# Hybrid encoder block on one core: the conv branch's layer norm in channels-by-tokens layout, attention scores over the allowed keys only

## The chip, the cores and the metric

The kernel runs on 1 core of one Trainium2 chip. TensorE (PE) multiplies matrices: it holds one operand as weights (the loads are the rows of PEld) and streams the other through, with results in PSUM, eight banks of 128 partitions by 512 fp32 numbers. VectorE (DVE), ScalarE (ACT) and GpSimd (POOL) work on tiles of up to 128 partitions in SBUF or PSUM. SyncE (SP) and ACT issue the DMAs, the copies between device memory and SBUF. Each engine works through its own instruction list in order and waits on semaphores of the others. The metric is the device time of one execution, in microseconds (us); lower is better.

## The reference

One layer of an encoder, for 1 sequence of 1024 tokens with 1024 features, in float32:

```python
h = rms_norm(x, norm1_g)
z = h @ w_in                                  # 2560 columns: a, gate, q, k, v, 512 each
# conv branch (512 channels)
u = a * sigmoid(gate)
y = depthwise_conv(u, dw_kernel) + dw_bias    # 31 taps over the tokens, centred
xc = y - mean(y, channels)
y = xc * rsqrt(mean(xc * xc, channels) + 1e-6) * ln_g + ln_b
conv_out = silu(y)
# attention branch: 8 heads of 64, tokens on a grid of 16 rows x 64 columns
q, k = rms_norm per head
# each query attends to a window of 8 rows x 16 columns, clamped inside the grid
s = q . k / 8 + rpb[row offset, column offset]
attn_out = softmax(s) @ v
x = x + concat(conv_out, attn_out) @ w_out
h = rms_norm(x, norm2_g)
x = x + (silu(h @ w_gate) * (h @ w_up)) @ w_down      # 2816 hidden features
```

A key column can be used by a query only if it lies in the query's 16 columns, and likewise for rows; all other keys of a tile get a table entry of -1e30 in place of the bias and so a weight of 0.

## The kernel before

The order of every engine's instructions is the order in which the program is written (the scheduler is set to manual). PE work is interleaved by hand: `proj` and the input projections emit their matmuls, and after each three of them (a `mac`: an fp32 product as three products of split halves, hi·hi, hi·lo, lo·hi, L115 to L117) call `weave()`, which pops one closure from the list `woven` and emits it there. `split` (L107 on ACT, L111 on DVE or POOL) makes the hi and lo halves that `mac` takes: ACT rounds to hi, the other engine subtracts.

SBUF buffers come from pools by size: `G` 21 of 128x1024, `H` 7 of 128x4096, `R` 4 of 128x1024, `ST` 5 of 128x512, `SM` 12 small ones. PSUM has `mm` (4 banks), `tp` (2 banks) and `cv` (one tile of 2 banks). A tile that takes a buffer waits until the readers of the tile before it in that buffer are done. A DMA also waits until the DMA issued eight before it on its completion semaphore has landed.

The stages, in us of the profiled execution: first norm, k projection and the GLU (0 to 95); q projection, the bias tables and most of the conv taps (95 to 200); the value projection with the first scores (200 to 235.3); the attention loop (235.3 to 294.8); the rest of attention, the conv layer norm and the first part of the output projection (294.8 to 337.4); the second part (337.4 to 420); the FFN's up half (420 to 730) and down half (730 to 1029).

*Conv branch.* `u[c]` (c = 0 to 3) is a tile of 128 channels by 1024 tokens. DVE does most of the taps (L363, one instruction of 128x1009 or more for each tap and channel block), ACT and POOL the others (L385 to L389), and DVE adds both sums into `u[c]` (L368). In the layer norm, `conv_T(t)` (L824) turns 128 tokens with 4 transposes of `u` on PE into one tile `y` of tokens by 512 channels; DVE takes its mean and variance (L831, L832), ACT the root (L833), DVE the reciprocal (L843); ACT (L852) or DVE (L848) writes the normalised rows `xh`. `conv_silu(h, c)` (L857) turns 4 blocks of `xh` back with 4 transposes into `z`, 128 channels by 512 tokens; ACT applies gain, bias and Silu (L858), and `split` makes `cm[h]`, the left operand of the output projection `pj`. There are 8 `conv_T` and 8 `conv_silu`, each a closure in `woven`, popped between the matmuls of the output projection whose left operand is the attention output `at`.

*Attention.* A step `s_` is 128 queries (8 grid rows of 16 columns), `order` lists the 8 steps by half of the rows `rh` and column block `cb`. `WIN` gives the key columns of each block: 24, 32, 32, 24. `AR` = 12 is the number of key rows. An index `i` is a step and a pair of heads, 32 in all. `score_mm(i)` (L680) makes 2 products of 128 queries by 12·24 = 288 or 12·32 = 384 keys; `score_max` (L693) adds the table `tab` and takes the row maximum; `score_exp` (L698) is ACT's exponential with its sum; `score_norm` (L707 on DVE, L709 on POOL) scales; `flip(i)` (L720) makes 3 transposes for each head (keys onto partitions, 4 grid rows of keys, 96 or 128, at a time); `flip_out` copies them to SBUF (L727 on DVE, L729 on ACT); `weigh(i)` (L739) multiplies with the value rows `vw`. Each weighing product and each score product shows as two matmul records.

*Value rows.* The value projection writes `vd` in device memory (8 tiles of 128 tokens, by ACT's queue, L447); `load_vw` (L660) reads windows of it back through SP's queue, one DMA for each grid row in a group of 4, of 24 or 32 tokens, for one or two groups at a time.

Of the kernel before, what the change touches and what calls it, by code (L numbers as in the profile page):

```python
# [25 lines left out]
AR = 12  # L26
SIDE = (16, 17, 18, 19, 20, 21, 22)
WIN = ((0, 24, 8), (8, 32, 0), (24, 32, 0), (40, 24, 0))
# [42 lines left out]
def build(ctx, tc, a):  # L71
# [206 lines left out]
    t1 = [dr.tile([NH, 16, 15, ncol], F32, name=f"t1{ty}") for ty, ncol in enumerate((24, 32, 24))]  # L278
    tf = {(rh, ty): dr.tile([16, 8, NH, AR * t1[ty].shape[-1]], F32, name=f"tf{rh}{ty}")
# [71 lines left out]

    def conv_taps():
        for c in range(4):
# [14 lines left out]
            dve.tensor_tensor(uc, acc, aside[c][0], OP.add)  # L368
            yield True
# [132 lines left out]
    aside_dma = []  # L502

    def bias_tables():
        neg = G("neg")
        pool.memset(neg, NEG)

        def fill1(ty):
            n = 15 * t1[ty].shape[-1]
            nc.sync.dma_start(t1[ty].rearrange("h j u b -> (h j) (u b)"), neg[:, :n])  # L510

        def fill2(rh, ty):
            n = 3 * AR * t1[ty].shape[-1] if ty != 1 else 2 * AR * 32
            for o in range(0, NH * AR * t1[ty].shape[-1], n):
                w = min(n, NH * AR * t1[ty].shape[-1] - o)
                nc.sync.dma_start(tf[rh, ty].rearrange("j i h c -> (j i) (h c)")[:, o:o + w], neg[:, :w])
# [6 lines left out]
        def rows_of(rh, ty, i):  # L523
            ncol = t1[ty].shape[-1]
# [113 lines left out]
    def table(rh, ty):  # L638
        n = AR * t1[ty].shape[-1]
        src = tf[rh, ty].rearrange("j i h c -> (j i) (h c)")  # L640
        if rh == 0 and ty == 0:
            parts = [(G(f"tab{k}")[:, :n * min(3, NH - 3 * k)], 3 * k) for k in range(3)]
# [10 lines left out]

    def load_vw(cb, *gs):
        c0, ncol, _ = WIN[cb]
        if gs[0] % 2 == 0:
            vwt[cb, gs[0] // 2] = G(f"vw{cb}{gs[0]}").rearrange("p (g d) -> p g d", d=512)
        w = vwt[cb, gs[0] // 2]
        for r in range(4):
            nc.sync.dma_start(w[r * ncol:(r + 1) * ncol, gs[0] % 2:gs[-1] % 2 + 1, :],  # L660
                              vd.rearrange("(g r c) d -> r c g d", r=4, c=GW)[r, c0:c0 + ncol, gs[0]:gs[-1] + 1, :])
        for g in gs:
            vw[cb, g] = w[:4 * ncol, g % 2, :]


# [4 lines left out]

    def score_mm(i):
# [3 lines left out]
        c0, ncol, _ = WIN[cb]  # L675
        s2 = cv(f"s{i}") if i > 0 and i % 2 == 0 else None
        out = []
        for hh in range(2):
            s = (mm(f"s{i}{hh}") if s2 is None else lr(s2)[hh])[:, :AR * ncol]
            pe.matmul(s, qT[hh * HD:(hh + 1) * HD, hp, t * P:(t + 1) * P],  # L680
                      k4[hh * HD:(hh + 1) * HD, hp, rh * 4:rh * 4 + AR, c0:c0 + ncol], start=True, stop=True)
# [3 lines left out]
    def score_max(i, hh, s):  # L685
        s_, hp = divmod(i, 4)
        rh, cb = order[s_]
        if i not in es:
            et[i] = G(f"e{i}").rearrange("p (h n) -> p h n", h=2)
            es[i] = et[i][:, :, :AR * WIN[cb][1]]  # L690
# [21 lines left out]
    def flip(i):  # L712
        s_, hp = divmod(i, 4)
        m = 4 * WIN[order[s_][1]][1]
# [3 lines left out]
        for hh, pt in enumerate(pp[i]):  # L718
            for g in range(3):
                pe.transpose(pt[:m, g * P:(g + 1) * P], es[i][:, hh, g * m:(g + 1) * m], ident)  # L720

    def flip_out(i, hh=None):
        m = 4 * WIN[order[i // 4][1]][1]
        w = et[i][:m, :, :384]
        pTs[i] = [w[:, h].rearrange("p (n q) -> p n q", q=P) for h in range(2)]
        if hh is None:
            dve.tensor_copy(w, cvs[i].rearrange("p (h n) -> p h n", h=2)[:m, :, :384])  # L727
        else:
            act.copy(w[:, hh], pp[i][hh][:m, :384])  # L729

    def weigh(i):
# [4 lines left out]
        for g in range(3):  # L736
            for hh in range(2):
                c = (2 * hp + hh) * HD
                pe.matmul(os_[s_][hh * HD:(hh + 1) * HD, hp], vw[cb, rh + g][:, c:c + HD], pTs[i][hh][:, g],  # L739
                          start=g == 0, stop=g == 2)  # L740
# [42 lines left out]
    load_vw(0, 0, 1)  # L783
# [15 lines left out]
    load_vw(0, 3)  # L799
    load_window(3)  # L800
    tab[1, 3] = table(1, 2)
# [19 lines left out]
    def conv_T(t):  # L821
        y = cv(f"y{t}")[:, :512] if t in (0, 3) else tp(f"y{t}")
        for c in range(4):
            pe.transpose(y[:, c * P:(c + 1) * P], u[c][0][:, t * P:(t + 1) * P], ident)  # L824
        return y

    cs = {}

    def conv_stats(t, y):
        st6, mv, sd = SM(f"bs{t}", 6), SM(f"bm{t}", 2), SM(f"bd{t}", 1)  # L830
        dve.bn_stats(st6, y)  # L831
# [706 lines left out]
```

## Time and profile before

| | |
|---|---|
| median of 3 runs | 1031.15 us (1030.76 to 1031.35) |
| the profiled execution's own time | 1030.59 us |
| its span | 1028.9 us |
| granted TensorE clock | 1.00 throughout |
| PE busy | 1022.9 us (99%) |
| PEld busy | 854.4 us (83%) |
| DVE / ACT / POOL busy | 771.8 / 479.4 / 447.7 us |
| attention loop, 235.3 to 294.8 | PE busy 59.19 of 59.50 us |
| conv norm and projection, 294.8 to 337.4 | PE busy 42.24 of 42.60 us |

The span runs from the first to the last instruction on the core; the time of a run is 1.7 us longer in the profiled execution. Matmuls are pipelined: a 128x512 one is shown with 389 ns and its successor starts some 230 ns after it, so a cost on PE is read from start to start. "Idle before" in a row is the time in which the engine stood still ahead of it, with what ended that.

### The profile page before, as it was taken

The page shows a single profiled execution, that of the slowest core. Times are in us where ns is not written, and L with a number is a line of the kernel's source. Part 1 is how long each engine was busy: PE and PEld are TensorE (multiplying, and loading weights), DVE is VectorE, ACT ScalarE, POOL GpSimd, SP SyncE. Part 2 cuts the span into 40 slices and gives each one's busy share as a digit, 9 for nine tenths or more (in the row PEclk, how much of TensorE's full clock was granted, in tenths as well). Part 3 has the DMA queues.
Part 4 walks back from the last instruction along what each step waited for, and adds up shares of the span by engine and source line. Part 5 has one row for each costly group of instructions (what it writes and reads, how often), then busy time and mean ns, then how long its engine had stood idle before and what let it go on. Part 6 is the DMA issues. An engine that isn't in the chain of part 4 may idle for free.

```text
span 1028.9 us, 15157 instructions
## 1 busy us (share of the span) xinstructions
PE 1022.9 (99%) x5334; PEld 854.4 (83%) x5334; DVE 771.8 (75%) x1226; ACT 479.4 (47%) x1045; POOL 447.7 (44%) x353
## 2 busy tenths in 40 slices
PE   9999999999999999999999999999999999999998
PEld 8888888877787888888888888888888888888887
DVE  5788897896755475987787787787777767758874
ACT  7565348836866345523334333343342543433432
POOL 1036674534641347257667667567565200003210
PEclk9999999999999999999999999999999999999999
DMA  9426781337403621133334424434341696634641
GB/s 351 163 69 213 224 257 55 114 120 236 127 22 123 236 92 41 41 113 115 131 123 154 154 89 148 154 119 139 132 153 63 233 363 234 223 103 124 209 129 41
DMA packets 75084, 152.53 MB, mean 148 GB/s; under 512 B 13824, under 2 KB 22784, under 8 KB 74368
## 3 DMA queue, kind: packets, MB, share of 16 engines
q1 hardware_dynamic: 72992, 148.21, 42.8%
q10 hardware_dynamic: 2016, 3.36, 0.9%
q8 instruction: 42, 0.69, 0.3%
q14 instruction: 34, 0.28, 0.1%
HBM read 112.38 MB, written 44.76 MB: 153 GB/s over the span
## 4 chain that ended last, share of the span: by engine, by line
PE 96%; DVE 2%; ACT 1%; POOL 1%; issue 0%; POOLq 0%; ACTq 0%; DVEq 0%
PE B L116 5%; PE B L115 5%; PE B L117 5%; PE z L115 4%; PE z L117 4%; PE z L116 4%; PE D L115 4%; PE D L116 4%; PE D L117 4%; PE gl L115 3%; PE gl L116 3%; PE gl L117 3%; PE pj L116 3%; PE pj L115 3%; PE pj L117 3%; PE p L720 2%
## 5 line engine op out<-in xcount | busy, mean ns | idle before, releaser
L363 DVE SCALAR_TENSOR_TENSOR cv<-u,par,cv 128x1009 f32<-128x1009 f32 (+14 forms) x92 | 117.5, 1277 | 2.3
L389 POOL TENSOR_TENSOR pa<-pa,pr 128x1022 f32<-128x1022 f32 (+5 forms) x24 | 58.0, 2418 | 48.9 <-ACT pr L388 32.9
L107 ACT CAST op<-sr 128x512 fp32r<-128x512 f32 x77 | 47.7, 620 | 58.0 <-PE B2d L117 24.4
L1481 POOL TENSOR_TENSOR ou<-ou,resm 128x512 f32<-128x512 f32 x8 | 12.5, 1565 | 139.5 <-DVE ou L1472 126.1
L111 DVE TENSOR_TENSOR op<-sr,op 128x512 fp32r<-128x512 f32 x77 | 58.6, 761 | 17.4 <-ACT op L107 17.3
L709 POOL TENSOR_SCALAR e<-e,rs 128x288 f32<-128x288 f32 (+1 forms) x64 | 34.0, 548 | 41.6 <-DVE rs L707 39.9
L107 ACT CAST op<-wd 128x512 fp32r<-128x512 f32 x54 | 33.6, 622 | 27.8 <-DVE wd L1376 18.1
L698 ACT ACTIVATE e<-e,mx 128x288 f32<-128x288 f32 (+1 forms) x64 | 36.6, 573 | 18.7 <-DVE mx L693 16.8
L1028 DVE TENSOR_TENSOR ts<-gu,ts 128x512 f32<-128x512 f32 x38 | 42.8, 1127 | 0.7
L693 DVE CUSTOM_DVE_ANT_0 e<-s,tab 128x288 f32<-128x288 f32 (+1 forms) x64 | 28.7, 504 | 13.6 <-PE s L680 13.6
L111 DVE TENSOR_TENSOR op<-wd,op 128x512 fp32r<-128x512 f32 x54 | 38.0, 704 | 1.1
L980 POOL TENSOR_TENSOR sq<-sq,sq 128x512 f32<-128x512 f32 x12 | 17.1, 1425 | 45.8 <-ACT sq L976 45.7
L1289 DVE TENSOR_TENSOR g<-D,g 128x512 f32<-128x512 f32 x22 | 15.2, 690 | 23.1 <-PE D L117 23.1
L416 ACT ACTIVATE sq<-z,r 128x64 f32<-128x64 f32 x96 | 28.3, 330 | 4.9 <-PE z L117 4.9
L1266 ACT ACTIVATE D<-D 128x512 f32<-128x512 f32 x22 | 12.8, 582 | 33.6 <-DVE D L1265 33.6
L388 ACT ACTIVATE pr<-u,par 128x1022 f32<-128x1022 f32 (+5 forms) x24 | 27.1, 1139 | 1.6 <-ACT vs L446 1.2
L720 PEld LDWEIGHTS p<-ident,e 128*96 128x96 f32 (+1 forms) x192 | 20.5, 133 | 6.9 <-POOL e L709 6.3
L115 PE MATMUL B2d<-op 128*128 128x512 f32 x66 | 25.8, 391 | 0.0
L116 PE MATMUL B2d<-op 128*128 128x512 f32 x66 | 25.7, 389 | 0.0
L117 PE MATMUL B2d<-op 128*128 128x512 f32 x66 | 25.7, 389 | 0.0
L870 DVE TENSOR_TENSOR xT<-pj,xT 128x512 f32<-128x512 f32 x16 | 10.8, 687 | 19.1 <-PE pj L117 18.8
L739 PE MATMUL o<-e,vw 96*64 96x128 f32 (+1 forms) x384 | 24.7, 277 | 0.0
(1461 smaller groups left out, 3752.7 us busy)
## 6 DMA issues: line engine op xcount, KB each, us to landing
gu<-in_gu SPq DMA_DIRECT2D x44, 512.0 KB
sr<-sd SPq DMA_DIRECT2D x77, 256.0 KB
sd<-sd SPq DMA_DIRECT2D x22, 512.0 KB
wd<-in_wd SPq DMA_DIRECT2D x36, 256.0 KB
sd<-g SPq DMA_DIRECT2D x33, 256.0 KB
x<-in_x SPq DMA_DIRECT2D x8, 512.0 KB
xT<-in_xp SPq DMA_DIRECT2D x8, 512.0 KB
xd<-xT SPq DMA_DIRECT2D x16, 256.0 KB
```

The source lines that it names most:

```text
L107: act.copy(hi, src)
L111: eng.tensor_tensor(*[w[..., sl] for w in (lo, src, hi.bitcast(F32))], OP.subtract)
L115: pe.matmul(acc, lh, rh, start=start, stop=False, skip_group_check=True)
L116: pe.matmul(acc, lh, rl, start=False, stop=False, skip_group_check=True)
L117: pe.matmul(acc, ll, rh, start=False, stop=stop, skip_group_check=True)
L363: dve.scalar_tensor_tensor(acc[:, o], uc[:, i], dwk[:, c, t:t + 1], acc[:, o], OP.mult, OP.add)
L389: pool.tensor_tensor(pa[:, o], pa[:, o], pr[:, o], OP.add)
L693: dve.tensor_tensor_reduce(out=es[i][:, hh], in0=s[hh], in1=tab[rh, cb][2 * hp + hh], scale=-1.0, scalar=3.0e38, op0=OP.add, op1=OP.min, a ...
L698: act.activation(e, e, AF.Exp, bias=mx.pop((i, hh)), scale=-1.0, accum_out=sums[i][:, hh:hh + 1])
L709: pool.tensor_scalar(es[i][:, hh], es[i][:, hh], rs[:, hh:hh + 1], 1.0, op0=OP.mult, op1=OP.mult)
L720: pe.transpose(pt[:m, g * P:(g + 1) * P], es[i][:, hh, g * m:(g + 1) * m], ident)
L1028: (pool if (i, n) in ON_POOL else dve).tensor_tensor(o, l, r, OP.subtract)
```

## The change

*Conv layer norm.* The data stays channels by tokens. While the taps run, POOL adds the four `u[c]` into `cs` (`channel_sum`, 3 additions of 128x1024). `sum_split` splits `cs` into hi and lo. For each half `h` of the tokens: `conv_mean` multiplies both with a matrix of ones (2 matmuls of 128x512), which leaves the sum over all channels in every partition of a PSUM tile `mr`; `conv_dev` subtracts the mean from each `u[c]` on DVE (4 instructions of 128x512), squares on ACT (4), and adds the squares (1 addition on POOL, 2 on DVE); `conv_var` multiplies with a column of ones (4 small matmuls), then root on ACT and reciprocal on DVE; `conv_rows` spreads the reciprocals over the partitions (4 transposes of a broadcast column) into `vr`; `conv_norm` multiplies on DVE (4 for each half); `conv_silu` is Silu and `split`, without transposes. A dictionary `slots` places them in `woven`.

*Attention.* `AR` is 11 rows for the upper half and 12 for the lower, `WIN` has 23, 31, 31, 24 columns. The score products have 253, 276, 264, 288, 341, 372, 341, 372 columns in the order of the steps (before: 288 four times, 384 four times), and so have the table, exponential and scaling. Step 0 (253 keys) is cut into groups of 128 and 125 keys in place of three groups of 96; the others keep three. Transposed blocks are rounded up to a multiple of 32 keys; POOL sets the added columns of `e` to 0 (28 small memsets, `score_max`), and added value rows are loaded from `zd`, a device tile of zeros. Step 0 has value rows of its own (`load_first`); `value_rows` loads a run of 23 or 31 rows as 16 and the rest. The table of step 0 comes in 2 loads in place of 3.

```diff
-AR = 12
+AR = (11, 12)
-WIN = ((0, 24, 8), (8, 32, 0), (24, 32, 0), (40, 24, 0))
+WIN = ((0, 23), (8, 31), (24, 31), (40, 24))
...
+    def channel_sum(c):
+        if c == 1:
+            cs.append(G("cs"))
+        if c > 0:
+            pool.tensor_tensor(cs[0], u[0][0] if c == 1 else cs[0], u[c][0], OP.add)
+
+    def sum_split(h):
+        if h == 0:
+            cr.extend([G("crh", F32R), G("crl", F32R), ST("onesr", F32R)[:, :P]])
+            dve.tensor_scalar(cr[2], ident, 0.0, 1.0, op0=OP.mult, op1=OP.add)
+        split(*[w[:, h * 512:(h + 1) * 512] for w in cr[:2] + cs])
...
             dve.tensor_tensor(uc, acc, aside[c][0], OP.add)
+            channel_sum(c)
...
+    def value_rows(w, at_, g, src, n):
+        m = n if n % 8 == 0 else 16
+        for o in range(0, n, m):
+            e = min(n, o + m)
+            nc.sync.dma_start(w[at_ + o:at_ + e, g, :], src[o:e])
...
+        if n > 4 * ncol:
+            nc.sync.dma_start(w[4 * ncol:n, gs[0] % 2:gs[-1] % 2 + 1, :], zd[:n - 4 * ncol, :len(gs), :])
...
+    def groups(s_):
+        n, m = width(s_), P if s_ == 0 else 4 * WIN[order[s_][1]][1]
+        return [slice(o, min(o + m, n)) for o in range(0, n, m)]
...
+            if n < end:
+                pool.memset(et[i][:, :, n:end], 0.0)
...
-            for g in range(3):
-                pe.transpose(pt[:m, g * P:(g + 1) * P], es[i][:, hh, g * m:(g + 1) * m], ident)
+            gs = groups(i // 4)
+            m = whole(gs[0].stop)
+            for g, k in enumerate(gs):
+                pe.transpose(pt[:m, g * P:(g + 1) * P], et[i][:, hh, k.start:k.start + m], ident)
...
-    load_vw(0, 0, 1)
+    load_first()
+    load_vw(0, 1)
     load_vw(0, 2)
...
-    def conv_T(t):
...
+    def conv_mean(h):
+        cw["m", h] = tp(f"mr{h}")
+        for n, w in enumerate(cr[:2]):
+            pe.matmul(cw["m", h], cr[2], w[:, h * 512:(h + 1) * 512], start=n == 0, stop=n == 1)
+
+    def conv_dev(h):
+        sq = []
         for c in range(4):
-            pe.transpose(y[:, c * P:(c + 1) * P], u[c][0][:, t * P:(t + 1) * P], ident)
...
+            w = of(c, h)
+            dve.scalar_tensor_tensor(w, cw["m", h], -1.0 / 512, w, OP.mult, OP.add)
+            sq.append(ST(f"sd{h}{c}"))
+            act.activation(sq[c], w, AF.Square)
+            if c == 1:
+                pool.tensor_tensor(sq[0], sq[0], sq[1], OP.add)
+        dve.tensor_tensor(sq[2], sq[2], sq[3], OP.add)
+        dve.tensor_tensor(sq[0], sq[0], sq[2], OP.add)
+        cw["s", h] = sq[0]
+
+    def conv_var(h):
+        if h == 0:
+            cw["r", 0], pt = lr(cv("vr0"))
         else:
...
+            pt = tp("vs1")
+        for t in range(4):
+            pe.matmul(pt[:, t:t + 1], cw["s", h][:, t * P:(t + 1) * P], one, start=True, stop=True)
+        sd, cw["v", h] = SM(f"cd{h}", 4), SM(f"cv{h}", 4)
+        act.activation(sd, pt[:, :4], AF.Sqrt, bias=eps, scale=1.0 / 512)
+        dve.reciprocal(cw["v", h], sd)
+
+    def conv_rows(h):
+        if h == 1:
+            cw["r", 1] = tp("vr1")
+        for t in range(4):
+            pe.transpose(cw["r", h][:, t * P:(t + 1) * P], cw["v", h][:, t:t + 1].to_broadcast([P, P]), ident)
+
+    def conv_norm(h, c):
+        dve.tensor_tensor(of(c, h), of(c, h), cw["r", h], OP.mult)
...
-    conv_stats(0, conv_T(0))
-    woven.extend([lambda: (weigh(31), evac_hi(7), evac_lo(7)), lambda: conv_stats(1, conv_T(1)), lambda: None])
-    for t in range(2, 8):
-        woven.extend([lambda t=t: conv_stats(t, conv_T(t)), lambda: None])
+    slots = {0: lambda: (weigh(31), evac_hi(7), evac_lo(7)), 2: lambda: (conv_mean(1), conv_dev(1)),
+             6: lambda: conv_var(0), 9: lambda: (conv_rows(0), [conv_norm(0, c) for c in range(4)]),
+             11: lambda: conv_var(1), 15: lambda: (conv_rows(1), act.activation(warm, eps, AF.Silu)),
+             16: lambda: (conv_silu(0, 0), conv_norm(1, 0))}
+    woven.extend(slots.get(n, lambda: None) for n in range(17))
```

What moves on PE, in the first part of the output projection: before, a transpose block of the conv output stands after every 6 matmuls of a projection (`pj` is the projection's PSUM tile, `at` the attention output, `wo04`, `wo06` the weights, `y` the tile of tokens by channels).

```order
L117 MATMUL pj_3272<-at_2385,wo04l 128x512
L824 MATMUL y_3279<-ident,u_539 128x128
L824 MATMUL y_3279<-ident,u_952 128x128
L824 MATMUL y_3279<-ident,u_1124 128x128
L824 MATMUL y_3279<-ident,u_1304 128x128
L115 MATMUL pj_3272<-at_2385,wo06h 128x512
```

After, in the next accumulator of the same stretch (`vr` is the PSUM tile of the spread reciprocals, half of tile `cv`; `cv` as its operand is the small tile of reciprocals; `vs` holds the sums of squares; `pj_3401` is the first accumulator in the PSUM tile of 2 banks that `vr` was in):

```order
L118 MATMUL pj_3371<-at_2434,wo04l 128x512
L919 MATMUL vr_3359<-ident,cv_3365 128x128 x4
L116 MATMUL pj_3371<-at_2434,wo06h 128x512
L117 MATMUL pj_3371<-at_2434,wo06h 128x512
L118 MATMUL pj_3371<-at_2434,wo06l 128x512
L116 MATMUL pj_3371<-at_2434,wo06h 128x512
L117 MATMUL pj_3371<-at_2434,wo06h 128x512
L118 MATMUL pj_3371<-at_2434,wo06l 128x512
L910 MATMUL vs_3392<-one,sd_3316 128x1 x4
L116 MATMUL pj_3401<-at_2435,wo04h 128x512
```

The transposes of `u` are gone; the spreading stands 6 matmuls ahead of the first product into `pj_3401`, and DVE's products that read `vr` stand between the two.

On DVE, the same stretch after the change (`mr` is the PSUM tile of channel sums, `sd` the squares, `cv_3365` and `cv_3398` the reciprocals of the two halves):

```order
L895 SCALAR_TENSOR_TENSOR u_1308<-mr_3312,u_1308 128x512
L900 TENSOR_TENSOR sd_3323<-sd_3323,sd_3326 128x512
L901 TENSOR_TENSOR sd_3316<-sd_3316,sd_3323 128x512
L913 RECIPROCAL cv_3365<-cd_3364 128x4
L922 TENSOR_TENSOR u_540<-u_540,vr_3359 128x512
```

The reciprocal of half 0, for which PE's spreading waits, stands behind all of `conv_dev` of half 1.

On SP, the loads of the value rows for the first two steps, before (`vd` is the value projection's device tile, `vw` the rows in SBUF, `tab`, `tf` the tables):

```order
L647 DMA tab_1976<-tf_118 128x2304
L660 DMA vw_2088<-vd 24x2x512 x4
L660 DMA vw_2093<-vd 24x512 x8
L660 DMA vw_2185<-vd 24x2x512 x4
```

and the middle of them after, from the end of step 0's own rows (`vwf`) on:

```order
L678 DMA vwf<-vd 16x512
L678 DMA vwf<-vd 7x512
L707 DMA vwf<-zd 3x512
L678 DMA vw_2119<-vd 16x512
L678 DMA vw_2119<-vd 7x512
```

Where 12 DMAs stood for the first two steps (rows `vw_2088` and `vw_2093`), there are now 50: 23 for `vwf`, and 9 for each of three groups of `vw`.

More of the change, by code (lines that the diff above doesn't have):

```diff
@@ L735, in weigh @@
             os_[s_] = tp(f"o{s_}").rearrange("p (c q) -> p c q", c=4)
-        for g in range(3):
+        gs = groups(s_)
+        for g, k in enumerate(gs):
+            n = whole(k.stop - k.start)
+            v = vwt["first"][:, g, :] if s_ == 0 else vw[cb, rh + g]
             for hh in range(2):
                 c = (2 * hp + hh) * HD
-                pe.matmul(os_[s_][hh * HD:(hh + 1) * HD, hp], vw[cb, rh + g][:, c:c + HD], pTs[i][hh][:, g],
-                          start=g == 0, stop=g == 2)
+                pe.matmul(os_[s_][hh * HD:(hh + 1) * HD, hp], v[:n, c:c + HD], pTs[i][hh][:n, g],
+                          start=g == 0, stop=g == len(gs) - 1)
     def half(name):
@@ L854, in conv_silu, with of @@
[L854 to L862 removed]
+    cw = {}
+    def of(c, h):
+        return u[c][0][:, h * 512:(h + 1) * 512]
```

118 lines of the change are left out of this document (58 added, 60 removed).

## The prediction

> **What bounds the kernel now.** I read the busy shares first, then the chain that ended last, then what PE waits for, then the two stages that the change touches.
>
> ```profile
> PE 1022.9 (99%) x5334; PEld 854.4 (83%) x5334; DVE 771.8 (75%) x1226; ACT 479.4 (47%) x1045; POOL 447.7 (44%) x353
> ...
> PE 96%; DVE 2%; ACT 1%; POOL 1%; issue 0%; POOLq 0%; ACTq 0%; DVEq 0%
> ```
>
> ```profile
> PE up L274 <- POOL ones L270: 1.0, 1, 1.0
> ...
> PE s L680 <- DVE e L727: 0.3, 1, 0.3
> PE pj L116 <- DVE cm L111: 0.2, 1, 0.2
> ```
>
> ```profile
> 235.30:294.80 59.50, 59.19 (x606) 44.90 (x605) 44.28 (x160) 49.17 (x154) 34.63 (x63) 1.00 0.52 161
> 294.80:337.40 42.60, 42.24 (x288) 35.35 (x287) 20.70 (x47) 26.29 (x46) 7.84 (x12) 1.00 0.21 79
> ```
>
> The chain is 96% PE, no wait of PE is longer than 1.0 us, and in both touched stages (columns: length, then busy time of PE, PEld, DVE, ACT, POOL, then the clock) PE lacks 0.3 to 0.4 us. So a microsecond of PE work removed there ends the program a microsecond sooner, if no wait takes its place; everything after 337.4 is PE work that the change leaves as it is.
>
> The Trainium skill, in "Perfetto Trace Analysis", section "Identifying the Most-Contended Engine", says that matmul busy time is no good measure of TensorE's headroom, and names the busy share of the weight loads as one to use. By the 83% of PEld there would be room on PE. The rows of matmul starts below decide against that here.
>
> **Attention, fewer columns.** Score products stand back to back with transposes and weighing:
>
> ```profile
> 268.30 1.56 PE L680 MATMUL s<-kT,qT 64*128 64x384 f32 x8
> 269.79 1.53 PE L720 MATMUL p<-ident,e 128*128 128x128 f32 x12
> 271.25 1.53 PE L739 MATMUL o<-e,vw 96*64 96x128 f32 x24
> 272.71 1.56 PE L680 MATMUL s<-kT,qT 64*128 64x384 f32 x8
> ```
>
> ```profile
> 239.11 1.24 PE L680 MATMUL s<-kT,qT 64*128 64x288 f32 x8 [0.31 <-DVE e L727]
> 240.28 1.51 PE L720 MATMUL p<-ident,e 128*96 128x128 f32 x12
> ```
>
> From start to start, 8 records of 384 columns take 269.79 − 268.30 = 1.49 us, of 288 columns 1.17: 0.32/(8·96) = 0.42 ns for a column and record. The new widths are 35, 12, 24, 0, 43, 12, 43, 12 columns shorter, 181 in all, in 4 indices of 2 heads with 2 records each: 181·16·0.42 ns = 1.2 us less. A transpose is 1.46/12 = 0.122 us, a weighing record 1.46/24 = 0.061. Step 0 loses its third group: 8 transposes (1.0 us) and 16 records (1.0 us). Together −3.2 us, −3.0 if narrow columns cost a little more. The other steps' rounding to 32 keys costs PE nothing: a transposed block has 128 columns either way.
>
> **Attention, what it adds.** POOL's additions of `u` and 28 memsets, and SP's longer list of loads:
>
> ```profile
> L389 POOL TENSOR_TENSOR pa<-pa,pr 128x1022 f32<-128x1022 f32 (+5 forms) x24 | 58.0, 2418 | 48.9 <-ACT pr L388 32.9
> ```
>
> ```profile
> 144.60 2.44 POOL L111 TENSOR_TENSOR w20l<-w20r,w20h 128x1024 fp32r<-128x1024 f32 x1
> 151.22 2.40 POOL L389 TENSOR_TENSOR pa<-pa,pr 128x1021 f32<-128x1021 f32 x1 [4.18 <-ACT pr L388]
> ```
>
> ```profile
> 228.62 0.99 POOL L709 TENSOR_SCALAR e<-e,rs 128x288 f32<-128x288 f32 x2 [14.23 <-DVE rs L707]
> ```
>
> ```profile
> 227.23 1.23 DVE L368 TENSOR_TENSOR u<-cv,pa 128x1024 f32<-128x1024 f32 x1
> ```
>
> ```profile
> 232.49 0.82 PE L720 MATMUL p<-ident,e 128*96 128x128 f32 x6
> ```
>
> Three additions at 2.42 us. Two fall into gaps of POOL such as the 4.18 us ahead of 151.22. The last must follow the last tap sum on DVE, 227.23 + 1.23 = 228.46, and stands ahead of step 0's first scaling, which then ends near 228.46 + 2.42 + 0.9 = 231.8; the transposes that need it start at 232.49. Hidden by 0.7 us. If that cover goes, PE waits up to 1 us there.
>
> The value rows. On SP, today's loads: six that wait for nothing, the first that waits for the last value tile with ACT's write of that tile, and the whole stretch of them. On PE, the first weighing.
>
> ```profile
> 239.00 2.37 SPq L660 DMA_DIRECT2D vw<-vd  x6
> ```
>
> ```profile
> 236.14 0.33 ACTq L447 DMA_DIRECT2D vd<-vs  x1
> ```
>
> ```profile
> 238.19 0.30 SPq L660 DMA_DIRECT2D vw<-vd  x1
> ```
>
> ```profile
> 229.37 12.83 SPq L660 DMA_DIRECT2D vw<-vd  x14
> ```
>
> ```profile
> 237.93 0.88 PE L739 MATMUL o<-e,vw 96*64 96x128 f32 x12
> ```
>
> An issue takes 2.37/6 = 0.40 us, a transfer 238.19 − 236.14 = 2.05 us to its landing. The first load of the stretch at 229.37 follows the landing of value tile 5 (grid rows 10 and 11); in the new list 20 of the 50 DMAs need only earlier tiles, and 30 follow: 21 of them (rest of step 0, second and third group) until 229.4 + 21·0.40 = 237.8, the last 9 until 241.4, landed at 243.4. Step 0's own rows are issued by 230.6 and wanted by PE at 237.93; the last group is wanted by step 1's first weighing, near 244.3 (a round of the narrow loop is 1.17 + 1.46 + 1.46 = 4.1 us, so the transposes of 240.28 come again at 244.4 and the weighing behind them at 245.8, less the 1.5 us of PE work that go before it). So the slack is under 1 us. ACT shares the completion semaphores: its write of the last value tile must wait for a piece that lands near 237, which holds the exponentials behind it in ACT's list by up to 1.2 us. And DVE's copy already ends PE's 0.31 us wait at 239.11. I take 0.5 us of new waits for this start; the ends are 0 and 1.3. Later loads (4 groups of 9) are issued more than 20 us ahead of their use.
>
> **Conv norm, what it removes.** A block of four transposes between projection matmuls:
>
> ```profile
> 309.11 0.40 PE L116 MATMUL pj<-at,wo04h 128*128 128x512 f32 x1
> 309.34 0.40 PE L117 MATMUL pj<-at,wo04l 128*128 128x512 f32 x1
> 309.57 0.60 PE L824 MATMUL y<-ident,u 128*128 128x128 f32 x4
> ...
> 310.24 0.39 PE L116 MATMUL pj<-at,wo06h 128*128 128x512 f32 x1
> ```
>
> Two matmul steps take 309.57 − 309.11 = 0.46 us; from 309.34 to 310.24, with the block in between, 0.90. The block costs 0.44 us and there are 16 (8 `conv_T`, 8 `conv_silu`): −7.0 us. The silu half's waits go too, since its chain loses two PE trips:
>
> ```profile
> 322.21 0.49 PE L115 MATMUL pj<-cm,wo00h 128*128 128x512 f32 x1
> 322.94 0.50 PE L116 MATMUL pj<-cm,wo00h 128*128 128x512 f32 x1 [0.23 <-DVE cm L111]
> ...
> 326.38 0.47 PE L115 MATMUL pj<-cm,wo00h 128*128 128x512 f32 x1
> 326.98 0.50 PE L116 MATMUL pj<-cm,wo00h 128*128 128x512 f32 x1
> ```
>
> 322.94 − 322.21 is 0.73 where a step is 0.23, and 326.98 − 326.38 is 0.60: 0.9 us in both, counted as gone.
>
> **Conv norm, what it adds on PE.** The means are 4 matmuls of 128x512, 4·0.23 = 0.9, and 0.2 for changing between operands: 1.1. The sums of squares are the same products that the second norm makes:
>
> ```profile
> 363.24 0.39 PE L117 MATMUL pj<-cm,wo00l 128*128 128x512 f32 x1
> 363.46 0.95 PE L985 MATMUL ss<-one,sq 128*128 128x1 f32 x8
> ...
> 364.60 0.40 PE L116 MATMUL pj<-cm,wo02h 128*128 128x512 f32 x1
> ```
>
> 1.36 us from 363.24 to 364.60, 0.46 without: 0.9 each, 1.8 for both halves. Two spreadings at 0.44 are 0.9. Sum +3.8.
>
> **Its chain on the other engines.** Durations:
>
> ```profile
> L997 DVE SCALAR_TENSOR_TENSOR xT<-xT,par,rw 128x512 f32<-128x512 f32 x16 | 11.1, 740 | 2.2 <-PE rw L993 2.2
> L1028 DVE TENSOR_TENSOR ts<-gu,ts 128x512 f32<-128x512 f32 x38 | 42.8, 1127 | 0.7
> L1265 DVE TENSOR_TENSOR D<-D,u 128x512 f32<-128x512 f32 x22 | 15.2, 691 | 0.2
> ```
>
> ```profile
> L976 ACT ACTIVATE sq<-xT 128x512 f32<-128x512 f32 x16 | 10.1, 635 | 25.1 <-DVE xT L870 25.1
> ```
>
> PE's places are counted from the new order with 0.23 us a matmul, on the old time axis. Half 0's means come at 301.5, done at 302.1; DVE needs 4·0.7 us for the deviations, ACT 0.64 behind them, then two additions of 0.69: half 0 is through at 307. After one split for the attention output half 1 follows, its means long there: 307.75 + 4·0.7 + 0.64 + 2·0.69 = 312.5. Only then DVE takes the reciprocal of half 0, near 312.7; PE comes to the spreading at 313.2. The four products that read `vr` end at 316.5, and PE comes to `pj_3401`, which takes over that PSUM tile, at 315.95: a wait of 0.6 us. If the additions take the 1.13 us of L1028 (two SBUF inputs with POOL busy) in place of 0.69, four of them put 1.8 us more on this chain and both waits together come to about 2. Lower end 0.4. I take 1.0, since POOL is idle for most of this stretch but does add squares in it. What follows (spreading of half 1, eight Silus at 0.75 and splits) has PE ahead of it by less than a microsecond nowhere that I find; late next would be `cm` of half 0 for the first conv matmul.
>
> On this the Trainium skill, "SBUF — State Buffer", section "Who interferes with whom", speaks against the change: a DVE instruction with two SBUF inputs and a GpSimd instruction that reads SBUF exclude each other for a whole instruction. The trace agrees for L1028 (1127 against 691 ns), not for the taps:
>
> ```profile
> L363 DVE SCALAR_TENSOR_TENSOR cv<-u,par,cv x92: 1262/1277/1290, 56.4 to 225.9; 128x1009 f32<-128x1009 f32 x8, 128x1010 f32<-128x1010 f32 x8, 128x1011 f32<-128x1011 f32 x8, 128x1012 f32<-128x1012 f32 x8
> ```
>
> These take 1262 to 1290 ns, all 92, though 24 POOL additions of 2.4 us run in the same stretch. By the rule the three channel sums could hold DVE for 7.3 us, and the sum below would still have PE as its bound until the scores begin; by the row they hold it for nothing, and I go by the row.
>
> **The sum.** Against the profiled execution's 1030.59 us: −3.2 (attention) + 0.5 (its start) − 7.0 − 0.9 + 3.8 + 1.0 (conv norm) = −5.8. The median shown, 1031.15, is 0.6 higher; −5.8 from it gives 1025.3. The terms' ends: attention −3.0 to −3.2, start 0 to 1.3, conv −3.8 to −2.1; the whole −3.8 to −7.0, so 1024.1 to 1027.4.
>
> **Rivals.** (a) *The conv chain is longer than drawn.* Both halves go through DVE one after the other, and PE waits at the spreading, at `pj_3401` and at the first `cm`. At 1.13 us for all two-input DVE work (16 instructions at +0.44) the chain grows by 7 us; half of it before `pj_3401`, less 0.5 already counted, is 3 us of new waits: 1028.3. For it speaks L1028, against it 691 ns at L1265 and POOL's 7.84 us of 42.60.
>
> (b) *The loads of value rows are late, and the kernel is slower.* In place is SP's list from 229.4 on. If an issue with its turn on a completion semaphore took 0.80 us (the 14 DMAs of 12.83 us, 0.92 each, are the upper row, most of it waits for data) in place of 0.40, the last of 30 would be issued at 253.4 and landed at 255.4, 11.1 us after it is wanted: 1031.15 − 5.8 + 11.1 = 1036.5. Slower than before begins where PE loses the 5.8 us: 229.4 + 30·x + 2 = 244.3 + 5.8, that is x = 0.62 us. Against it: the six DMAs at 239.00 run at 0.40 with others under way.
>
> (c) *It does not do what it says.* The PE work that goes in the attention loop was cover for ACT (49.17 of 59.50 busy) and DVE, so a wait takes its place, and only the conv part shows: −3.1 + 0.5 = −2.6, 1028.6. Against it: the loop's softmax work shrinks by the same columns.
>
> (d) *Both (a) and (c) in part, within 0.2% of no change*: 1030.5.
>
> **How the numbers follow.** 0.2%, about 2.1 us, is what a measurement of this kernel can tell from no change: below 1029.1 is faster, above 1033.2 slower. Forecast 0.60; (a) 0.13; (c) 0.09; (d) 0.08; (b) 0.10. Faster 0.82, same 0.08, slower 0.10. The range takes in the forecast's own (1024.1 to 1027.4), rivals (a) and (c), and below it 1 us for waits that I counted and that may not come (those of the start and the conv chain): 1023.2 to 1029.0.
>
> **What would show it.** Right: PE busy in the attention loop 3 us lower with its idle time under 1.5 us; no `conv_T`; the stretch from the last attention step to the first conv matmul some 3 us shorter; a PE wait near `pj_3401` for DVE's `u` of 0.5 to 1 us; the part behind it as long as before. Wrong: PE waiting at step 1's weighing for a DMA; PE idle at `vr` for over 2 us; DVE's additions at 1.1 us; or a part after 337 that has grown, which I hold for excluded since its instructions and order are the same.

## The result and the profile after

The changed kernel takes 1025.20 us (1024.54 to 1025.61, 4 runs) against 1031.25 us (1030.76 to 1031.69, 4 runs): ratio 0.9940, 95% interval 0.9928 to 0.9953, 6.0 us faster. Its profiled execution took 1025.28 us with a span of 1023.6. The two views that answer to the first ones of before, of the changed kernel:

```profile
PE 1017.4 (99%) x5274; PEld 850.2 (83%) x5274; DVE 775.4 (76%) x1217; ACT 480.9 (47%) x1043; POOL 461.6 (45%) x389
...
PE 94%; DVE 2%; ACT 2%; issue 1%; POOL 1%; DVEq 0%; POOLq 0%; ACTq 0%
```

```profile
PE up L275 <- POOL ones L271: 1.1, 1, 1.1
PE pj L116 <- DVE u L922: 0.5, 1, 0.5
...
PE pj L116 <- DVE xT L936: 0.2, 1, 0.2
```

PE does 5.5 us less and is still the chain. Two waits are new: the 0.5 us for the products that read the spread reciprocals (`u`, L922) and 0.2 us for the residual add (`xT`, L936). The attention loop, the first part of the output projection and the part behind it up to the second norm's row transposes (columns as before):

```profile
235.81:293.23 57.42, 57.21 (x583) 43.43 (x582) 42.78 (x160) 47.67 (x154) 35.16 (x85) 1.00 0.54 167
293.23:331.90 38.67, 37.95 (x253) 32.39 (x251) 25.43 (x38) 29.89 (x44) 13.58 (x16) 1.00 0.24 88
331.90:360.68 28.78, 28.71 (x129) 23.28 (x130) 12.29 (x17) 9.33 (x13) 7.93 (x6) 1.00 0.61 220
```

The loop lost 2.0 us of PE work and has as little idle time as before (0.2 us). The projection's first part is 4.0 us shorter although PE idles 0.7 us in it. To see where each microsecond went, the starts of the same matmuls in both traces (us; the last column takes off the 0.90 us by which the fourth projection matmul of the whole program already starts later, a start that differs between profiles of identical instructions: 5.64 before, 6.54 after, 6.34 and 6.19 in two runs below):

| matmul | before | after | difference, corrected |
|---|---|---|---|
| first score of the attention loop | 235.31 | 235.81 | −0.40 |
| first `pj<-at,wo04h`, behind the loop | 294.77 | 293.23 | −2.44 |
| first `pj<-cm,wo00h`, conv output used | 322.21 | 320.63 | −2.48 |
| first `pj<-at,wo` of the next output block | 337.41 | 331.90 | −6.41 |
| second norm's first row transpose `rw` | 365.76 | 360.68 | −5.98 |

The steps from row to row are firm: the attention loop is 57.41 to 57.43 us long in this and in four later profiles of the same loop. The first row is not. By the same correction it comes out anywhere between −0.43 and +0.27 in seven later profiles whose PE work up to there is that of the changed kernel.

So attention gave 2.0 us in the loop and, by this table, 2.4 with what stands ahead of it. The conv norm gave 4.0 in the part where it stands, and 0.4 of that was lost again behind it. Inside the first half of the conv part the removed transposes and the added products balance; all the gain comes in the second half, where seven of the eight `conv_silu` have lost their transposes (the first one stands in the first half).

### The profile page after: what moved, and what is told of

Its sections match the earlier page's. It is cut to its first block, busy times and chain, and to the rows that moved or that the text cites. A ratio compares the mean times of both kernels' runs of the same rounds, so it can differ in the third digit from the quotient of the medians.

```text
span 1023.6 us, 15128 instructions
## 1 busy us (share of the span) xinstructions
PE 1017.4 (99%) x5274; PEld 850.2 (83%) x5274; DVE 775.4 (76%) x1217; ACT 480.9 (47%) x1043; POOL 461.6 (45%) x389
## 4 chain that ended last, share of the span: by engine, by line
PE 94%; DVE 2%; ACT 2%; issue 1%; POOL 1%; DVEq 0%; POOLq 0%; ACTq 0%
PE B L116 5%; PE B L117 5%; PE B L118 5%; PE z L116 4%; PE z L118 4%; PE z L117 4%; PE D L116 4%; PE D L117 4%; PE D L118 4%; PE gl L118 3%; PE gl L117 3%; PE gl L116 3%; PE pj L116 2%; PE pj L118 2%; PE pj L117 2%; PE p L775 2%
## 5 line engine op out<-in xcount | busy, mean ns | idle before, releaser
L753 ACT ACTIVATE e<-e,mx 128x341 f32<-128x341 f32 (+5 forms) x64 | 35.3, 553 | 18.1 <-DVE mx L748 18.1
L1097 DVE TENSOR_TENSOR ts<-gu,ts 128x512 f32<-128x512 f32 x38 | 42.9, 1129 | 0.7
L764 POOL TENSOR_SCALAR e<-e,rs 128x341 f32<-128x341 f32 (+5 forms) x64 | 32.9, 528 | 22.1 <-DVE rs L762 21.6
L748 DVE CUSTOM_DVE_ANT_0 e<-s,tab 128x341 f32<-128x341 f32 (+5 forms) x64 | 27.2, 481 | 13.1 <-PE s L731 12.9
L116 PE MATMUL B2d<-op 128*128 128x512 f32 x66 | 25.8, 391 | 0.0
L775 PEld LDWEIGHTS p<-ident,e 128*128 128x128 f32 (+1 forms) x184 | 19.7, 135 | 6.7 <-POOL e L764 5.1
L936 DVE TENSOR_TENSOR xT<-pj,xT 128x512 f32<-128x512 f32 x16 | 10.8, 686 | 19.0 <-PE pj L118 18.8
L775 PE MATMUL p<-ident,e 128*128 128x128 f32 (+1 forms) x184 | 23.9, 277 | 0.0
```

The source lines that it names most:

```text
L116: pe.matmul(acc, lh, rh, start=start, stop=False, skip_group_check=True)
L753: act.activation(e, e, AF.Exp, bias=mx.pop((i, hh)), scale=-1.0, accum_out=sums[i][:, hh:hh + 1])
L764: pool.tensor_scalar(es[i][:, hh], es[i][:, hh], rs[:, hh:hh + 1], 1.0, op0=OP.mult, op1=OP.mult)
L775: pe.transpose(pt[:m, g * P:(g + 1) * P], et[i][:, hh, k.start:k.start + m], ident)
L1097: (pool if (i, n) in ON_POOL else dve).tensor_tensor(o, l, r, OP.subtract)
```

## Experiments

Each kernel ran beside the kernel before on the same chip.

**1. Attention alone, and the conv norm alone.** The hunks of the diff on attention, bias tables and value rows on the kernel before; then those on the layer norm.

> The attention part of the change alone, with the conv layer norm of before. By the prediction's terms: -3.2 for shorter score products and the third group of step 0, +0.5 for new waits at the start of the loop, so 2.7 us below the kernel before, near 1028.5. By rival (c), the PE work that went was cover for ACT and DVE: PE idle in the loop grows by about as much, and the time is within 0.7 us of before. If the two parts are independent, this gain and that of conv_only add up to the whole change's 6.0.

Measured: 1029.01 us (ratio 0.9977, interval 0.9967 to 0.9986), 2.4 us below its 1031.37.

> The conv layer norm of the change alone, with the attention of before. By the prediction's terms: -7.0 - 0.9 + 3.8 + 1.0 = -3.1, near 1028.1; the wait at the first product into the tile that held the spread reciprocals is 0.5 to 1 us. By the trace of the changed kernel rather -3.5, of which some 0.7 us are lost again behind the conv block, where the residual add on DVE stands behind late splits. By rival (a), new waits of 3 us or more: 1030 or above.

Measured: 1027.97 us (0.9967, 0.9954 to 0.9979), 3.4 below. 2.4 + 3.4 = 5.8 against 6.0 for the whole: within the noise, some 1 us in each of the three, the parts are independent. In the conv-only trace PE has the two new waits and the loop of before:

```profile
PE pj L115 <- DVE u L877: 0.5, 1, 0.5
...
PE pj L115 <- DVE xT L891: 0.2, 1, 0.2
```

```profile
236.29:295.75 59.46, 59.15 (x606) 44.88 (x605) 44.24 (x160) 49.07 (x154) 34.59 (x63) 1.00 0.53 161
295.75:334.36 38.61, 37.92 (x252) 32.35 (x251) 25.12 (x38) 29.87 (x44) 13.82 (x16) 1.00 0.23 88
```

Rivals (a) and (c) of the prediction fall: the conv chain has no 3 us of new waits, and the attention work that went was not a cover.

**2. Step 0 in three groups again.**

```diff
-        n, m = width(s_), P if s_ == 0 else 4 * WIN[order[s_][1]][1]
+        n, m = width(s_), 4 * WIN[order[s_][1]][1]
...
-            v = vwt["first"][:, g, :] if s_ == 0 else vw[cb, rh + g]
+            v = vw[cb, rh + g]
...
-    load_first()
-    load_vw(0, 1)
+    load_vw(0, 0, 1)
```

> The changed kernel with step 0 in three groups of 92 keys, as the other steps, and its value rows loaded as for the others (18 DMAs fewer at the start). By the prediction's terms 8 transposes of 0.122 and 16 weighing records of 0.061 us come back: +1.9 us, less what the longer rounds hide of the two waits at the start of the loop (0.43 and 0.2 in the changed kernel, 0.3 before): +1.5 to +1.9. If the two-group step only traded work for waits, +0.5 or less.

Measured: 1026.11 us (0.9950, 0.9937 to 0.9962), 0.9 above the changed kernel, less than the 1.5 to 1.9 expected. In the traces the attention loop alone, from its first score to the first projection matmul behind it, takes 58.51 us here (235.32 to 293.83) and 57.42 in the changed kernel: 1.1 us for 6 transposes and 16 weighing records, 0.73 + 0.98 = 1.7 us by the prediction's prices (the other 2 transposes stand ahead of the loop). The remaining 0.6 was lost again. The loop's first rounds in the changed kernel, then in this one:

```profile
238.12 0.80 PE L798 MATMUL o<-e,vwf 128*64 128x128 f32 x8
239.04 1.20 PE L731 MATMUL s<-kT,qT 64*128 64x276 f32 x8
...
241.55 1.09 PE L798 MATMUL o<-e,vwf 128*64 128x128 f32 x16
242.74 1.16 PE L731 MATMUL s<-kT,qT 64*128 64x264 f32 x8
```

```profile
237.89 0.88 PE L798 MATMUL o<-e,vw 96*64 96x128 f32 x12
239.08 1.20 PE L731 MATMUL s<-kT,qT 64*128 64x276 f32 x8 [0.31 <-DVE e L783]
```

Weighing lost 0.2 of the 0.6. In the first round 8 records are 8·0.061 = 0.49 us of work, and the scores start 0.92 us after them, 0.43 more. With three groups it is much the same: 12 records are 0.73, and the scores start after 1.19, 0.46 more. In the second round 16 records are 0.98, and the scores start after 1.19, 0.21 more, where with three groups they wait for nothing (24 records, 1.47 us). The scores share a PSUM tile with the transposed weights, which DVE must copy out first (`e`, L783).

The transposes lost the other 0.4: 8 take 1.18 us (from 236.94 to the weighing at 238.12) and not 8·0.122 = 0.98, and 10 take 1.38 (240.17 to 241.55) and not 1.22. In the changed kernel the weights of the second index's transposes are loaded just behind the end of one of DVE's maxima:

```profile
237.33 0.08 DVE L748 DVE_READ_ACCUMULATOR2_ANT mx<- 128x1 f32 x1
237.53 0.42 PEld L775 LDWEIGHTS p<-ident,e 128*128 128x128 f32 x4 [0.17 <-issue]
```

So a wait for DVE is likely there too, but the profile names no releaser, and no run took it away.

**3. How close the value rows' loads are: pieces of 8 rows.**

```diff
-        m = n if n % 8 == 0 else 16
+        m = n if n % 8 == 0 else 8
```

> The changed kernel with value rows loaded in pieces of 8 rows in place of 16 and the rest. By the SP rows of the changed kernel (9 issues from 231.29 to 234.50, 0.36 us each) 43 DMAs in place of 30 follow the landing of value tile 5 near 230; the last is issued near 245.4 and lands near 247.4, where PE wants it at 245.8: PE waits about 1.5 us for a DMA at step 1's first weighing, and the time is 1 to 2 us above the changed kernel. If the issue rate on SP is not what limits these loads, there is no such wait and the time is the changed kernel's.

Measured: 1030.33 us (0.9991, 0.9981 to 1.0000), 5 us above the changed kernel and not 1 to 2. The changed kernel's SP rows, with 0.36 us an issue and the last of the 30 at 240.67:

```profile
231.29 2.77 SPq L678 DMA_DIRECT2D vw<-vd  x8
...
234.50 2.77 SPq L678 DMA_DIRECT2D vw<-vd  x8
...
240.67 0.29 SPq L693 DMA_DIRECT2D vw<-zd  x1
```

its ACT around the write of the last value tile:

```profile
235.92 0.69 ACT L462 ACTIVATE vs<-z,r 128x512 f32<-128x512 f32 x1 [3.07 <-PE z L118]
236.94 0.33 ACTq L463 DMA_DIRECT2D vd<-vs  x1
```

and with pieces of 8 the waits of PE, and what ACT stood still for at the same place:

```profile
PE p L775 <- ACT e L785: 2.9, 2, 2.6
PE o L798 <- DMA vw<-zd: 1.3, 1, 1.3
...
PE o L798 <- DMA vw<-vd: 0.7, 1, 0.7
```

```profile
240.44 0.33 ACTq L463 DMA_DIRECT2D vd<-vs  x1
240.82 0.53 ACT L753 ACTIVATE e<-e,mx 128x276 f32<-128x276 f32 x1 [4.67 <-DMA vw<-vd]
```

The last load was issued at 246.81, where 245.4 had been reckoned. What I had not reckoned into this run is the larger part: ACT's write of the last value tile waited for one of SP's loads on the same completion semaphore, until 240.44 where in the changed kernel it starts at 236.94, and the exponentials and copies behind it in ACT's list with it. PE waited 2.9 us for a copy of ACT's, and 2.0 us for value rows. The mechanism of rival (b) is real; the changed kernel passes this place with a hold of 0.33 us, from the end of the copy at 235.92 + 0.69 = 236.61 to the issue at 236.94. Its last load, issued at 240.67, was also less close than the prediction had it: with 2.05 us to its landing it was there by 242.7, and step 1's first weighing came to its rows at 245.76.

**4. Whole rows in one DMA.** The same line with `m = n`: 23 or 31 rows in one DMA, some 40 DMAs fewer.

> The changed kernel with each run of 23 or 31 value rows loaded by one DMA. By the theory that the loads are hidden with 2 us to spare, the time is the changed kernel's within 0.5 us, with SP through about 5 us earlier. If the number of DMAs costs PE time through waits on completion semaphores (ACT's write of the last value tile), the first weighing steps come earlier and up to 0.5 us is gained. If a DMA of 23 rows lands much later than one of 16, PE waits at a weighing and it is slower.

Measured: 1099.95 us (1.0664, 1.0650 to 1.0679). 75 us slower than the changed kernel with fewer DMAs and the same bytes. The waits of PE and a stretch of SP:

```profile
PE o L798 <- DMA vw<-vd: 48.5, 3, 22.2
PE o L798 <- DMA vw<-zd: 8.6, 2, 6.9
PE p L775 <- ACT e L785: 7.1, 1, 7.1
```

```profile
277.57 5.04 SPq L678 DMA_DIRECT2D vw<-vd  x1
282.65 5.13 SPq L693 DMA_DIRECT2D vw<-zd  x1
287.82 15.54 SPq L678 DMA_DIRECT2D vw<-vd  x4
303.41 5.12 SPq L693 DMA_DIRECT2D vw<-zd  x1
```

Nearly every issue here ends some 5 us after the one before, held until an earlier load on the same completion semaphore has landed. That a longer piece could land later had been weighed, but nothing of this size. A load of 31 rows for two groups is 31·4096 bytes = 124 KB, so some 25 GB/s for all of them together; those of the kernel before, 24 or 32 rows for two groups, were issued every 0.40 to 0.48 us where nothing else held them.

**5. 17 rows and 15 rows.** The number of rows was the only suspect left, so the size of a piece was moved by one in each direction (`else 17`, `else 15`).

> The changed kernel with value rows in pieces of 17 and the rest (23 = 17 + 6, 31 = 17 + 14) in place of 16 and the rest; as many DMAs as in the changed kernel. Theory from the run with whole rows (31 rows of 4 KB one after the other every 5.14 us, 124 KB / 5.14 us = 24 GB/s, 23 rows of 2 KB every 1.9 us): a DMA whose row count has no divisor up to 16 but 1 is moved one at a time by one DMA engine. 17 rows should then take 1.4 us of 2 KB and 2.8 us of 4 KB; 12 of the first near 230 to 247 and 16 of the second, 45 us, until about 294: PE waits for value rows and the time is 5 to 20 us above the changed kernel. Rival: whole rows were slow by the bytes in one DMA; then 17 rows are like 16, and the time is the changed kernel's.

Measured: 1060.64 us (1.0285, 1.0256 to 1.0315); 35 us slower than with 16, with as many DMAs of nearly the same size. More than the 5 to 20 expected.

```profile
PE o L798 <- DMA vw<-vd: 14.0, 3, 10.9
PE o L798 <- DMA wo16r<-in_wo: 6.4, 1, 6.4
PE p L775 <- ACT e L785: 5.4, 1, 5.4
```

```profile
236.00:300.00 64.00, 44.40 (x382) 32.36 (x378) 28.51 (x111) 32.27 (x107) 22.68 (x56) 0.81 0.33 112
```

The three waits are 25.8 us; most of the rest is the granted clock, 0.81 in this stretch where PE idles a third of the time, so that what it does takes longer (PE busy is 1026.7 us here, 1017.4 in the changed kernel). The weighing products read no `wo16r`; that row names the load of another tile on a completion semaphore that value rows use too.

> The changed kernel with value rows in pieces of 15 (23 = 15 + 8, 31 = 15 + 15 + 1). By the same theory 15, 8 and 1 rows are moved by 15, 8 and 1 engines, and the time is the changed kernel's within 1 us (16 DMAs more for the later windows, which have slack). If odd counts as such were slow, PE would wait as with whole rows.

Measured: 1025.74 us (0.9945, 0.9923 to 0.9968): the changed kernel's time. Odd counts are not slow, nor 16 DMAs more among the later loads; loads of 17, 23 and 31 rows are slow, and those of 7, 8, 15, 16, 24 and 32 are not (the 14 rows that stand beside 17 can't be told apart from them). The Trainium skill says how this comes about, in "DMA: Bandwidth & Descriptors", section "Why a DMA increments its semaphore by 16 and not by 1": the DMA engines that share a transfer are the largest number up to 16 that divides its slowest dimension, and they are the lowest-numbered ones. By that rule 17, 23 and 31 rows, which are prime, go through one engine, and all such loads through the same one. The runs agree in every count that they tell apart. That one engine moves them is the page's word; the rows show the times, 5.1 us for 124 KB one after the other.

**6. The two new waits of the conv norm.** Both come from the trace of the changed kernel. The Silu half there and in the kernel before (ACT's cast and DVE's subtraction for `cm`; first changed, then before):

```profile
L108 ACT CAST cm<-u 128x512 fp32r<-128x512 f32 x8 | 9.0, 1129 | 0.3
```

```profile
L112 DVE TENSOR_TENSOR cm<-u,cm 128x512 fp32r<-128x512 f32 x8 | 8.8, 1100 | 5.5 <-ACT cm L108 5.5
```

```profile
L107 ACT CAST cm<-z 128x512 fp32r<-128x512 f32 x8 | 4.7, 588 | 0.3
L111 DVE TENSOR_TENSOR cm<-z,cm 128x512 fp32r<-128x512 f32 x8 | 5.5, 691 | 9.7 <-ACT cm L107 9.7
```

Shape, type and output are the same, and both read tokens with a stride of 64; only the source moved from PSUM (`z`) to SBUF (`u`). SBUF alone is not what costs: an unstrided cast of the same shape from SBUF takes 619 ns in the changed kernel. POOL is not the cause either, since it runs nothing from 313.4 to 336.5, where all eight stand.

```profile
L108 ACT CAST op<-sr 128x512 fp32r<-128x512 f32 x77 | 47.6, 619 | 57.5 <-PE B2d L118 26.8
```

So Silu was made to write to PSUM again; for the PSUM tiles to come free in order, the four products of half 1 also move ahead of the later Silus.

```diff
-        act.activation(w, w, AF.Silu, bias=lnb[:, c:c + 1], scale=lng[:, c:c + 1])
+        y = tp(f"z{h}{c}")
+        act.activation(y, w, AF.Silu, bias=lnb[:, c:c + 1], scale=lng[:, c:c + 1])
...
-        split(hi, lo, w.rearrange("p (i b j) -> p b j i", b=4, j=16), (dve,))
+        split(hi, lo, y.rearrange("p (i b j) -> p b j i", b=4, j=16), (dve,))
...
-             16: lambda: (conv_silu(0, 0), conv_norm(1, 0))}
+             16: lambda: (conv_silu(0, 0), [conv_norm(1, c) for c in range(4)])}
```

> The changed kernel with the Silu's output in a PSUM tile, as before the change, and all four products of half 1 ahead of the later Silus (the PSUM turn needs that). In the changed kernel the cast and the subtraction that make cm read their rows with a stride from SBUF and take 1.13 and 1.10 us; before, from PSUM with the same stride, 0.59 and 0.69. Theory: it is SBUF with a stride that costs; here both fall back to about 0.6 and 0.7, ACT's chain of eight gets 4 us shorter, the waits of PE at the first output block after the conv block (0.28) and in the two blocks behind it (0.46 together) go, and the time is 0.5 to 0.8 us below the changed kernel. Rival: the durations come from POOL or DVE work beside them; then they stay at 1.1 and nothing is gained.

Measured: 1024.46 us (0.9933, 0.9921 to 0.9945).

```profile
L108 ACT CAST cm<-z 128x512 fp32r<-128x512 f32 x8 | 4.7, 588 | 0.3
```

```profile
L112 DVE TENSOR_TENSOR cm<-z,cm 128x512 fp32r<-128x512 f32 x8 | 5.5, 690 | 5.5 <-ACT cm L108 5.4
```

Both are back at 588 and 690 ns. From the first projection matmul behind the loop to the second norm's row transpose, this trace is 1.0 us shorter than the changed kernel's (359.50 − 293.09 against 360.68 − 293.23). The wait for `xT` is gone from PE's list, as it should be if the late splits had put DVE's residual add off and through it the next accumulators. The run moves the four products too, and what part of the 1.0 us is theirs is not shown. The Trainium skill, "SBUF — State Buffer", section "Door 1: The DMA port swizzle", says that accesses crossing from one 16-byte line of SBUF to the next pay a penalty; a stride of 64 numbers crosses at every one, and the trace agrees with a factor of 1.9 on ACT. It says the same of PSUM with lines of 8 bytes, for matmuls; for ACT and DVE the trace shows no penalty there (588 and 690 ns with the stride; the unstrided `at<-o` from PSUM takes 570 on ACT and 672 on DVE).

The other wait, ahead of `pj_3401`:

```profile
313.17 0.95 PE L910 MATMUL vs<-one,sd 128*128 128x1 f32 x8
314.60 0.47 PE L116 MATMUL pj<-at,wo04h 128*128 128x512 f32 x1 [0.49 <-DVE u L922]
```

```diff
         if h == 0:
-            cw["r", 0], pt = lr(cv("vr0"))
-        else:
-            pt = tp("vs1")
+            cw["s2"] = lr(cv("vs"))
+        pt = cw["s2"][h]
...
-        if h == 1:
-            cw["r", 1] = tp("vr1")
+        cw["r", h] = tp(f"vr{h}")
...
-             11: lambda: conv_var(1), 15: lambda: (conv_rows(1), act.activation(warm, eps, AF.Silu)),
+             10: lambda: conv_var(1), 15: lambda: (conv_rows(1), act.activation(warm, eps, AF.Silu)),
```

> The changed kernel with the spread reciprocals of both halves in the tp banks and both sums of squares in the two-bank tile, the second sum one slot earlier. Theory: the 0.62 us that PE loses ahead of the first product into that tile is DVE's reading of the spread reciprocals; it goes, and PE waits there for nothing (ACT's root is done by then): 0.4 to 0.6 us below the changed kernel, within its noise in the times, plain in the trace. Rival: the wait moves to ACT's root or to the second spreading, and nothing is gained.

Measured: 1023.98 us (0.9932, 0.9920 to 0.9944); the wait is gone from PE's list, and the same stretch is 0.7 us shorter (360.17 − 293.44). The median is 1.2 below the changed kernel's, where 0.4 to 0.6 had been expected.

> Both edits together. If they are independent, 0.9 to 1.4 us below the changed kernel, near 1024.0; no wait of PE over 0.3 us between the attention loop and the second norm.

Measured: 1023.46 us (0.9926, 0.9913 to 0.9940), the lowest median of all kernels here, 1.7 below the changed kernel's where 0.9 to 1.4 had been expected; the stretch is 1.7 us shorter than the changed kernel's (358.63 − 292.85). The list of PE's waits in this kernel:

```profile
PE up L275 <- POOL ones L271: 1.1, 1, 1.1
PE q41m L118 <- POOL qb4m L112: 0.5, 1, 0.5
PE D L116 <- DVE g L1337: 0.4, 1, 0.4
```

None of the conv norm is left in it. This is the version to keep: 8.0 us below the kernel before in its runs.

## Why the prediction was right

Forecast 1025.3 us, measured 1025.20; −5.8 forecast, −6.05 measured. The terms, each from its own measurement:

- *Score columns:* −1.2 forecast, of which 0.24 for step 0's products, which stand ahead of the loop. In the loop −1.0, and −0.95 measured (59.46 before, 58.51 with three groups).
- *Step 0's third group and the start of the loop:* −1.9 and +0.5, of which −1.7 and +0.5 in the loop; there −1.1 measured, so 0.6 of new waits. The size was right, the place only in part: DVE's copy ends 0.2 of them, as named, and 0.4 stand at the transposes, where the forecast had none. ACT's held write, which it had named first, was 0.33 us and cost PE nothing.
- *Conv norm, first half:* nine transpose blocks removed (eight `conv_T`, one `conv_silu`), −4.0, and +3.8 added with +1.0 of waits, so +0.8 forecast up to the first conv matmul; measured 0.0. Here the forecast was too dear: the means took 0.46 each with the transition and not 0.55, the first spreading waited for nothing, and the wait at `pj_3401` was 0.6, as drawn on the chain, where 1.0 had been taken. DVE's additions took 0.69 to 0.75 us and not 1.13. This accounts for 0.6 of the 0.8; the rest is open.
- *Conv norm, second half:* seven blocks, −3.1, and −0.9 of waits; measured −3.9 (−6.41 + 2.48).
- *Behind it:* held for excluded, measured +0.4. This step failed: "a part after 337 that has grown, which I hold for excluded since its instructions and order are the same". The instructions were the same, but DVE reached its residual adds late, because the splits of `cm` had become 1.1 us long (in the changed kernel the add at 331.07 stands behind a split that started at 330.05 and took 1.11). The prediction put the Silus at 0.75 us and named the splits without a price; the change of the source from PSUM to SBUF stood in the diff (`y.rearrange` to `w.rearrange`).

The errors cancel: the conv norm's first half cost 0.8 us less than forecast, the part behind it 0.4 more, and attention gave some 0.3 less (−2.4 against −2.7). The nearness of 0.1 us is luck; that no term is off by more than 0.8 is not.

Rivals: (a), the chain's new waits, came to 0.0 us at the spreading, 0.6 at `pj_3401` and 0.0 at the first `cm`; 0.4 came behind them. (b), late loads: the pieces of 8 show that late loads are not far off: 13 DMAs more ahead of step 1 cost 5 us. As forecast it did not come, since an issue took 0.36 us and not 0.62; but a larger danger at the same place, the row count of a piece, was not in the prediction at all. (c) and (d) did not come.

Of the two rules weighed, the choice against the first was borne out: PE's headroom of 17% by the weight loads was none, since the time followed PE's work stage by stage. On the second the forecast came out right for another reason than the one it gave. The channel sums on POOL did not lengthen the taps:

```profile
L378 DVE SCALAR_TENSOR_TENSOR cv<-u,par,cv 128x1009 f32<-128x1009 f32 (+14 forms) x92 | 117.5, 1277 | 2.3
```

But that is no evidence against the rule, which is on DVE instructions with two inputs in SBUF: the taps read `u` from SBUF and `cv` from PSUM. Where the rule applies, the trace before agrees with it. The mean of 1127 ns at L1028 is made of two kinds: 22 of the 38 have no POOL instruction beside them and take 679 to 693 ns; the 16 that start while POOL is in a subtraction take 1661 to 1784.

```profile
498.39 1.64 POOL L111 TENSOR_TENSOR qb6m<-qs6m,qb6m 128x512 fp32r<-128x512 f32 x1 [1.08 <-ACT qb6m L107]
498.80 1.78 DVE L1028 TENSOR_TENSOR ts<-gu,ts 128x512 f32<-128x512 f32 x1
```

So 1.13 us was the price of no single addition. In the changed kernel the four additions of squares, with both inputs in SBUF, escaped: POOL's instruction began after them or had 0.1 to 0.2 us left when they began.

## What to carry to other kernels

Where one engine is busy 99% with starts back to back, price a change by its start-to-start costs there, stage by stage, and treat each shortened stretch as cover taken from something: ask what DVE copy or ACT hold now ends the wait. Check for each operand that moves between SBUF and PSUM whether it is read with a stride. Before loading a run of rows, look at the count: pieces of 16 or 15 and the rest were in time here, and one row more than 16 in a piece cost 35 us.

## What the hardware showed that I had not expected

- 17 rows in place of 16 in a piece of a load: 1060.64 against 1025.20 us; 23 and 31 rows in one DMA: 1099.95. Such loads land one after the other, 5.1 us for 124 KB.
- A strided read of 128x512 fp32 by ACT: 588 ns from PSUM, 1129 ns from SBUF, where an unstrided cast from SBUF takes 619; DVE's subtraction 690 from PSUM against 1100 ns from SBUF.
- A DMA issue on ACT that waits for a transfer of SP's queue on a shared completion semaphore holds ACT's arithmetic too: 4.67 us with pieces of 8.
- With pieces of 17 the granted clock was 0.81 in the stretch of 64 us in which PE idled a third of the time, and the waits cost more than their length (35 us for 25.8). With pieces of 8, where PE waited 4.9 us in all, the profiled run kept 1.00 and lost 5 us.
